# RWKV time mixing on one core: a drain with two pairs of denominator banks and a log that runs one tile ahead, replaced by a drain with one pair of banks and the log and exponential of a tile in direct succession

## The chip, the cores and the metric

The kernel runs on one core of a Trainium2 chip. The metric is the device time of one execution in microseconds (us). Five engines work beside each other, each in its own program order: TensorE (PE, matmul, with its weight loads shown as PEld), VectorE (DVE), ScalarE (ACT), GpSimd (POOL) and SyncE (SP). SP, ACT and POOL also issue transfers between the on-chip memory (SBUF) and the main memory; the queues of those issues are shown as SPq, ACTq and POOLq. Matmul results lie in PSUM, eight banks of 128 x 512 float32.

## The reference

The inputs are `k` and `v` of shape (16, 2048, 256) and the vectors `w` (decay) and `u` (bonus) of length 256. For each of the 16 sequences and each of the 256 channels a recurrence runs over 2048 steps, and all of it is in float32:

```python
for t in range(seq_len):
    ww = u + kk; qq = max(pp, ww)
    e1, e2 = exp(pp - qq), exp(ww - qq)
    output[b, t] = (e1 * aa + e2 * vv) / (e1 * bb + e2 + 1e-08)
    ww = pp - w + kk; qq = max(ww, kk)
    e1, e2 = exp(ww - qq), exp(kk - qq)
    aa, bb, pp = e1 * aa + e2 * vv, e1 * bb + e2, qq
```

So each output is a ratio of a weighted sum of `v` (the numerator) to the sum of the weights (the denominator), and the state `aa, bb, pp` is carried from step to step.

## The kernel before

**Tiles.** The 2048 steps are cut into 16 chunks of 128 steps (`NST = 16`), and the 16 sequences into four groups of four. A tile `n` is one group in one chunk, so there are `NP = 64` tiles, numbered chunk by chunk: tile `n` belongs to chunk `n // 4`. A tile holds 128 steps (the partitions) by 1024 numbers (4 sequences x 256 channels), computed in two halves `i = 0, 1` of 512 columns.

**One tile's work.** `logs(n)` (PE) builds exponents from `k` in PSUM; `exps(n)` (ACT, L204) turns them into weights and writes them to a ring in SBUF, `EZR`, that has room for 12 tiles; `times_v(n)` (DVE, L214) multiplies them by `v`. `sums(n)` (PE, L238) adds up what the chunk contributes to the state. Ten turns later (`LAG = 10`) the output side of the same tile runs:

- `den(n)` (PE, L341): four matmuls of 512 columns, which leave the denominators of both halves in a pair of PSUM banks, `DENB` (banks 4 and 5).
- the reciprocal (ACT): the natural log of the pair into an SBUF tile `rd` (`den_log`, L346, 128 x 1024), and the exponential of the negated log, in place (`den_exp`, L349, 128 x 1024).
- `num(n, bank, i)` (PE, L358): two matmuls of 512 columns for each half, which leave the numerator in one bank.
- `mult(n, bank, i)` (DVE, L362): numerator times reciprocal, into `rd`.
- `store(n)` (SP, L365): `rd` (512 KB) to the output in main memory. There are eight `rd` tiles, so the log of tile `n` needs the store of tile `n - 8` to have landed.

**The state.** After the last tile of a chunk the state goes through a chain of small steps: `copy_sums` (out of PSUM), `turn` (PE, L255, a transposition by matmul), `state_logs` (ACT, L260), `state_frames`, `state_scan` and `state_offsets` (on DVE in the last chunk, L269 to L286), `state_weights` (ACT, L290), `state_chain` (DVE, L299 to L304), `turn_back` (PE, L320), and `inject` (DVE copy L326, then four transfers of 8 KB, L331), which writes the incoming state into rows of `EZR`. The output side of the next four tiles reads these rows: `den` needs the first two of the four transfers, `num` the other two. For the last chunk (`c = 15`) these are the tiles 60 to 63.

**Order.** All instructions are kept in the order of the program (`K(...)`), so each engine's queue is written out by hand. In the steady loop (`for n in range(LAG, NP)`) the small steps are slotted in by a table, `later`, of (turn, place, step), called by `small_work`. In the last turn of that loop `n = 63`, and the output side has come to tile `q = 53`.

**The drain.** What follows the loop handles the outputs of the tiles 53 to 63 and the state chain of chunk 15, with no loads and no weights left to compute. In the kernel before it is written out line by line:

- Denominators alternate between two pairs of banks (`dbank`: banks 2 and 3, or `DENB`), so that `den(n + 1)` is computed while the log of tile `n` still reads the other pair. Numerators go round three single banks (`nbank`: 0, 1 and 6).
- On ACT the log runs one tile ahead: log(n + 1), then exp(n), then log(n + 2), and so on. No two neighbours depend on each other.
- The steps of the state chain stand between the first few tiles at places of their own; `inject(c, SP)` issues its four transfers on SP's queue.
- The products and the store of a tile come as soon as its reciprocal is there (`outputs`): two products of 512 columns, then the store.
- Of tile 63 the log is taken whole; then, for each half, exponential, product, and two transfers of 128 KB, one on SP's queue and one on ACT's (L533). ACT issues its transfer of the first half ahead of the exponential of the second.

Of the kernel before, what the change touches and what calls it, by code (L numbers as in the profile page):

```python
# [7 lines left out]
F32 = mybir.dt.float32  # L8
# [3 lines left out]
ACT = mybir.ActivationFunctionType  # L12
# [3 lines left out]
def kernel(  # L16
# [14 lines left out]
    TC = 2 * HS  # L31
# [22 lines left out]
    def rows_of(x, n):  # L54
        c, p = divmod(n, 4)
        return x[4 * p:4 * p + 4, c * TC:(c + 1) * TC, :].rearrange("n t d -> t n d")
# [114 lines left out]
    def ez(n):  # L171
        return EZR[:, :, n % RING]
# [6 lines left out]
    def logs(n):  # L179
        km = KM[n].rearrange("p (i n) d -> p i (n d)", i=2)  # L180

        def rows(q):
            for i in range(2):
                g = 32 * (2 * q + i)
                K(PE.matmul(half(n, q)[:, i, :], CO[g:g + 32, :],  # L185
                            WU[g:g + 32, :].unsqueeze(1).broadcast_to([32, 2, Dm]), start=True, stop=False,
                            tile_position=(g, 0), skip_group_check=True))

        def steps(q):
            for i in range(2):  # L190
                K(PE.matmul(half(n, q)[:, i, :], (NLE, NLZ)[q], km[:, i, :], start=False, stop=True,  # L191
                            skip_group_check=True))

        rows(0)
        rows(1)
        steps(0)
        steps(1)
# [33 lines left out]
    def sums(n):  # L231
        c, p = divmod(n, 4)
        t = MISC[:, 0:Dm]
        for o in range(2):
            x = 24 - 16 * o - 2 * p
            for j in range(4):
                q, i = divmod(j, 2)
                K(PE.matmul(t[32 * j:32 * j + 32, :], mats["OH"][:, x:x + 32],  # L238
                            ez(n)[:, 2 * q, i, Dm * o:Dm * o + Dm],
                            start=p == 0 and o == 0, stop=p == 3 and o == 1,  # L240
                            tile_position=(0, 32 * j), skip_group_check=True))
# [79 lines left out]
                        skip_group_check=True))  # L321
        st[c, "CT"] = t

    def inject(c, queue=POOL):
        cb = small.tile([128, 128], BF16, tag="cb", name="cb")
        K(DVE.tensor_copy(cb, st.pop((c, "CT"))))  # L326
        r0 = 4 * c % RING
        for q in range(2):
            for h in range(2):
                r, x = HS * h + HS - 1, 32 * (2 * q + h)  # L330
                K(queue.dma_start(  # L331
                    out=EZR[r:r + 1, 2 * q, r0:r0 + 4, :, :].rearrange("o p i (b x) -> o (p i b) x", b=4),
                    in_=cb[x:x + 32, :]))


    RD = {}

    def den(n, bank=DENB):
        for m, q in (("L", 0), ("Id", 1)):
            for i in range(2):  # L340
                K(PE.matmul(bank[:, i, :], mats[m], ez(n)[:, q, i, :], start=q == 0, stop=q == 1,  # L341
                            skip_group_check=True))

    def den_log(n, bank=DENB):
        RD[n] = rpool.tile([128, 2, D], F32, tag="rd", name="rd")
        K(SC.activation(RD[n], bank, ACT.Ln, scale=RS))  # L346

    def den_exp(n, i=slice(0, 2)):
        K(SC.activation(RD[n][:, i, :], RD[n][:, i, :], ACT.Exp, scale=-1.0))  # L349

    def recip(n, between):
        den_log(n)
        between()
        den_exp(n)

    def num(n, bank, i):
        for m, q in (("LN", 2), ("IdN", 3)):
            K(PE.matmul(bank, mats[m], ez(n)[:, q, i, :], start=q == 2, stop=q == 3, skip_group_check=True))  # L358

    def mult(n, bank, i):  # L360
        rd = RD[n]
        K(DVE.tensor_mul(rd[:, i, :], bank, rd[:, i, :]))  # L362

    def store(n):
        K(SP.dma_start(out=rows_of(out, n), in_=RD.pop(n).rearrange("p i (n d) -> p (i n) d", n=2)))  # L365

    later = {}
    for c in range(NST):
        s = 4 * c + 3
        plan = [(s + 1, "act" if s + 1 < LAG else "recip", copy_sums), (s + 1, "pe", turn),  # L370
                (s + 2, "act", state_logs), (s + 2, "mid", state_frames), (s + 2, "scan", state_scan), (s + 2, "scan", state_offsets),
                (s + 3, "recip", state_weights), (s + 3, "chain", state_chain),
                (s + 4, "nums", turn_back), (s + 4, "mid", inject), (s + 4, "mid", state_next)]
        if c == 0:
            plan = [(s + 1, "act", copy_sums), (s + 1, "pe", turn), (s + 1, "pe", state_logs),
                    (s + 1, "round", state_frames), (s + 1, "round", state_scan), (s + 1, "round", state_offsets),
                    (s + 2, "act", state_weights), (s + 2, "round", state_chain),
                    (s + 3, "pe", turn_back), (s + 3, "round", inject), (s + 3, "round", state_next)]
        if c == 1:
            plan = [(s + 1, "act", copy_sums), (s + 1, "pe", turn), (s + 2, "act", state_logs),  # L380
                    (s + 2, "round", state_frames), (s + 2, "round", state_scan), (s + 2, "round", state_offsets),
                    (s + 3, "recip", state_weights), (s + 3, "early", state_chain)] + plan[8:]
        if c == NST - 1:
            plan = []
        for slot, where, f in plan:
            later.setdefault((slot, where), []).append((f, c))

    def small_work(n, where):
        for f, c in later.pop((n, where), []):
            f(c)  # L390
# [35 lines left out]
    def inverses(n):  # L426
        q, qp = n - LAG, n - LAG - 1
        if qp >= 0:
            num(qp, NUMB, 1)

        sums(n - 1)
        if n + 1 < NP:
            recip(q, lambda: small_work(n, "recip"))

    for n in range(LAG, NP):

        q, qp = n - LAG, n - LAG - 1
        load(n + AHEAD)

        if qp >= 2:  # L440
            store(qp - 2)
        if qp >= 0:
            num(qp, NUMB, 0)
        den(q)
        small_work(n, "nums")
        exps(n)
        small_work(n, "act")
        if qp >= 0:
            mult(qp, NUMB, 0)
        small_work(n, "mid")  # L450
        if n == LAG:

            inverses(n)
            small_work(n, "early")
        if n + 2 < NP:
            round_k(n + 2)

        if n % 4 in (3, 0):
            cast_v(n)
        if n + 1 == NP:  # L460
            times_v(n)
        elif n % 4 < 2:
            cast_v(n + 1)
        if n > LAG:
            inverses(n)
        if qp >= 0:
            mult(qp, NUMB, 1)
        small_work(n, "scan")
        if n + 1 < NP:
            times_v(n)  # L470
            small_work(n, "chain")
            logs(n + 1)
        small_work(n, "pe")

    q, c = NP - LAG - 1, NST - 1
    dbank = lambda n: PS[:, 2:4, :] if (n - q) % 2 else DENB
    nbank = lambda n, i: PS[:, (0, 1, 6)[(2 * (n - q) + i) % 3], :]  # L480
    tile_num = lambda n, i: num(n, nbank(n, i), i)

    def outputs(n):
        for i in range(2):
            mult(n, nbank(n, i), i)
        store(n)

    den_log(q)
    den(q + 1, dbank(q + 1))
    sums(NP - 1)  # L490
    copy_sums(c)
    store(q - 2)
    store(q - 1)
    den_exp(q)
    den_log(q + 1, dbank(q + 1))
    tile_num(q, 0)
    turn(c)
    state_logs(c)
    den_exp(q + 1)
    den(q + 2, dbank(q + 2))  # L500
    den_log(q + 2, dbank(q + 2))
    tile_num(q, 1)
    mult(q, nbank(q, 0), 0)
    state_frames(c)
    state_scan(c)
    state_offsets(c)
    state_weights(c)
    mult(q, nbank(q, 1), 1)
    store(q)
    state_chain(c)  # L510
    den(q + 3, dbank(q + 3))
    for i in range(2):
        tile_num(q + 1, i)
    turn_back(c)
    inject(c, SP)
    outputs(q + 1)
    for n in range(q + 2, NP):
        if n + 1 < NP:
            den_log(n + 1, dbank(n + 1))
        if n + 2 < NP:  # L520
            den(n + 2, dbank(n + 2))
        for i in range(2):
            tile_num(n, i)
        if n + 1 < NP:
            den_exp(n)
            outputs(n)
    n, p = NP - 1, (NP - 1) % 4
    for i in range(2):
        den_exp(n, slice(i, i + 1))
        mult(n, nbank(n, i), i)  # L530
        for j, eng in ((0, SP), (1, SC)):
            b = 4 * p + 2 * i + j
            K(eng.dma_start(out=out[b, c * TC:(c + 1) * TC, :], in_=RD[n][:, i, Dm * j:Dm * j + Dm]))  # L533
    assert not later


# [28 lines left out]
```

## Time and profile before

| | us |
|---|---|
| median of 3 runs (lowest, highest) | 290.13 (289.65, 290.43) |
| the profiled execution, its own time | 289.65 |
| its span, first to last instruction | 288.0 |
| mean granted TensorE clock | 0.988 |
| busy: PE, DVE, ACT, POOL | 261.4, 262.3, 254.7, 105.2 |
| start of the log (L346) of tile 53, of tile 54 | 258.54, 260.56 |
| end of the last product (L362) | 284.15 |

The profile is one execution, read by a hardware profiler. A row of the timeline gives start and length in us, the engine, the line of the kernel, what is written from what, and in square brackets how long the engine had been idle and who released it. The rows of "windows" give a stretch, its length, each engine's busy time (with its number of instructions), the granted TensorE clock as a share of full speed, the busy share of the 16 DMA engines and the rate in GB/s. The page's second part cuts the span into 40 slices of 7.2 us and gives tenths of busy time for each. The profiled execution's time is 1.65 us more than its span.

### The profile page before, as it was taken

To read this page: it belongs to the slowest core of one execution; us is meant where nothing else is said; L and a number is where in the kernel's file an instruction comes from. 1 tells how busy PE (TensorE), PEld (TensorE's weight loads), DVE (VectorE), ACT (ScalarE), POOL (GpSimd) and SP (SyncE) were. 2 spreads that over 40 slices of the span, in tenths; PEclk is the share of its full clock that TensorE was granted. 3 is DMA by queue.
4 is the path that set the end of the run, shared out by engine and by line. 5 is a ranking of instruction groups with operands and counts; after the bars stand their busy time and mean duration, and the time that the engine had idled before them with its cause. 6 is when DMAs were issued, how large, how long until landed. Compare 5 with 4: busy or idle time off the path is not lost. (4 is left out here: it accounts for less than half of the span.)

```text
span 288.0 us, 5023 instructions
## 1 busy us (share of the span) xinstructions
PE 261.4 (91%) x1694; PEld 119.4 (41%) x1694; DVE 262.3 (91%) x463; ACT 254.7 (88%) x252; POOL 105.2 (37%) x208
## 2 busy tenths in 40 slices
PE   5997897999999999999999999899998989998990
PEld 1443443544444544435444444344344444433430
DVE  4698999999999999999999999998999999988863
ACT  2675678999999999999999989999998999998891
POOL 7000523352534454543525364460434435233000
PEclk9799999999999999999999999999999999999997
DMA  6999999999999999999999999999999999994697
GB/s 214 353 348 350 349 331 349 331 361 375 381 369 381 372 379 378 381 379 381 378 376 381 369 381 375 377 376 371 373 374 380 374 377 380 373 383 160 201 339 245
DMA packets 103587, 101.54 MB, mean 353 GB/s; under 512 B 4285, under 2 KB 103561, under 8 KB 103561
## 3 DMA queue, kind: packets, MB, share of 16 engines
q1 hardware_dynamic: 101336, 100.45, 102.6%
q0 software_dynamic: 1920, 0.50, 0.8%
q8 instruction: 13, 0.21, 0.3%
q10 hardware_dynamic: 304, 0.27, 0.3%
q14 instruction: 14, 0.11, 0.1%
HBM read 67.12 MB, written 33.55 MB: 350 GB/s over the span
## 5 line engine op out<-in xcount | busy, mean ns | idle before, releaser
L204 ACT ACTIVATE EZR<-PS 128x2048 bf16<-128x2048 f32 x54 | 101.2, 1875 | 7.5 <-PE PS L191 6.5
L362 DVE TENSOR_TENSOR rd<-PS,rd 128x512 f32<-128x512 f32 x128 | 87.0, 687 | 6.1 <-ACT rd L349 4.7
L214 DVE TENSOR_TENSOR EZR<-EZR,vb 128x2048 bf16<-128x2048 bf16 x64 | 78.1, 1220 | 2.2 <-ACT EZR L202 1.5
L349 ACT ACTIVATE rd<-rd 128x1024 f32<-128x1024 f32 (+1 forms) x65 | 67.9, 1047 | 2.7 <-DVE rd L362 1.8
L346 ACT ACTIVATE rd<-PS 128x1024 f32<-128x1024 f32 x64 | 65.7, 1026 | 0.8 <-PE PS L341 0.8
L358 PE MATMUL PS<-EZR,LN 128*128 128x512 bf16 x128 | 48.7, 381 | 12.2 <-DVE rd L362 8.4
L331 POOL DMA_DIRECT2D EZR<-cb x60 | 36.5, 614 | 52.1 <-DVE cb L326 45.4
L176 DVE CAST km<-kr 128x1024 fp32r<-128x1024 f32 x64 | 44.7, 699 | 6.9 <-DMA kr<-in_k_dram 6.4
L191 PE MATMUL PS<-km,NLE 128*128 128x512 f32 x128 | 47.5, 453 | 2.3 <-DVE km L176 2.2
L358 PE MATMUL PS<-EZR,IdN 128*128 128x512 bf16 x128 | 48.4, 378 | 0.0
L209 DVE CAST vb<-vr 128x1024 bf16<-128x1024 f32 x64 | 43.4, 694 | 0.7 <-DMA vr<-in_v_dram 0.7
L191 PE MATMUL PS<-km,NLZ 128*128 128x512 f32 x128 | 40.6, 398 | 0.0
L341 PE MATMUL PS<-EZR,Id 128*128 128x512 bf16 x128 | 38.1, 379 | 0.0
L341 PE MATMUL PS<-EZR,L 128*128 128x512 bf16 x128 | 38.1, 379 | 0.0
L185 PE MATMUL PS<-WU,CO 32*128 32x512 bf16 x256 | 27.2, 388 | 3.4 <-DVE WU L400 2.2
L269 POOL TENSOR_TENSOR F<-LL,LL 128x32 f32<-128x32 f32 x13 | 6.7, 515 | 61.9 <-ACT LL L260 61.9
L191 PEld LDWEIGHTS PS<-km,NLZ 128*128 128x128 f32 x128 | 24.4, 191 | 5.8
L191 PEld LDWEIGHTS PS<-km,NLE 128*128 128x128 f32 x128 | 19.3, 190 | 17.3 <-issue 12.9
L238 PE MATMUL PS<-EZR,OH 128*32 128x256 bf16 x512 | 26.1, 278 | 0.1
L202 ACT ACTIVATE EZR<-PS 128x1024 bf16<-128x1024 f32 x20 | 19.4, 1019 | 7.6 <-PE PS L191 7.6
L358 PEld LDWEIGHTS <-IdN 128*128 128x128 bf16 x128 | 12.5, 97 | 28.7 <-issue 26.3
L282 POOL TENSOR_TENSOR Q<-P,F 128x64 f32<-128x64 f32 x13 | 15.7, 1205 | 15.0 <-DVE P L273 15.0
(71 smaller groups left out, 200.0 us busy)
## 6 DMA issues: line engine op xcount, KB each, us to landing
kr<-in_k_dram SPq DMA_DIRECT2D x64, 512.0 KB, 8.3
vr<-in_v_dram SPq DMA_DIRECT2D x64, 512.0 KB, 8.3
out_dram<-rd SPq DMA_DIRECT2D x63, 512.0 KB, 8.1
EZR<-cb POOLq DMA_DIRECT2D x60, 8.0 KB, 5.3
out_dram<-rd SPq DMA_DIRECT2D x2, 128.0 KB, 2.7
out_dram<-rd ACTq DMA_DIRECT2D x2, 128.0 KB, 2.2
EZR<-cb SPq DMA_DIRECT2D x4, 8.0 KB, 1.9
wuf<-in_w_dram ACTq DMA_DIRECT2D x1, 8.0 KB
```

The costliest lines, as they stand in the source:

```text
L176: K(DVE.tensor_copy(km, kr_of.pop(n)))
L185: K(PE.matmul(half(n, q)[:, i, :], CO[g:g + 32, :], WU[g:g + 32, :].unsqueeze(1).broadcast_to([32, 2, Dm]), start=True, stop=False, tile_p ...
L191: K(PE.matmul(half(n, q)[:, i, :], (NLE, NLZ)[q], km[:, i, :], start=False, stop=True, skip_group_check=True))
L204: K(SC.activation(ez(n)[:, 0:2], PS[:, 0:4, :].rearrange("p (q i) x -> p q i x", q=2), ACT.Exp))
L209: K(DVE.tensor_copy(vb, vr))
L214: K(DVE.tensor_mul(ez(n)[:, 2:4], ez(n)[:, 0:2], vb.unsqueeze(1).broadcast_to([128, 2, 2, D])))
L331: K(queue.dma_start(out=EZR[r:r + 1, 2 * q, r0:r0 + 4, :, :].rearrange("o p i (b x) -> o (p i b) x", b=4), in_=cb[x:x + 32, :]))
L341: K(PE.matmul(bank[:, i, :], mats[m], ez(n)[:, q, i, :], start=q == 0, stop=q == 1, skip_group_check=True))
L346: K(SC.activation(RD[n], bank, ACT.Ln, scale=RS))
L349: K(SC.activation(RD[n][:, i, :], RD[n][:, i, :], ACT.Exp, scale=-1.0))
L358: K(PE.matmul(bank, mats[m], ez(n)[:, q, i, :], start=q == 2, stop=q == 3, skip_group_check=True))
L362: K(DVE.tensor_mul(rd[:, i, :], bank, rd[:, i, :]))
```

## The change

Up to the end of the steady loop the kernel stays as it is, apart from the output side of its last turn, which now calls the whole reciprocal of tile 53 there and issues `den(54)` at its end. The written-out drain goes, and a loop over `n = 64 ... 74` takes its place, with `q = n - 10` the tile whose reciprocal is taken and `qp = n - 11` the tile whose numerator is computed:

- one pair of denominator banks, `DENB`, for all tiles: `den(q + 1)` stands behind `num(qp)` and writes the pair that the log of tile `q` reads;
- `recip(q)`: log and exponential of one tile follow each other on ACT; for tile 63 they go half by half (log, exp, log, exp);
- numerators alternate between two pairs of banks, 0 and 1, or 2 and 3 (`H`), with one product of 1024 columns for both halves (tile 63: two of 512);
- the state chain of chunk 15 is slotted in by the table: `state_logs` behind the exponential of tile 54, `state_weights` behind that of tile 55, `state_chain` after it, `turn_back` behind `num(55)`, `inject` on POOL's queue, and the products of the tiles 54 and 55 behind the copy of `inject`;
- the transfers of the last tile are issued behind both of its exponentials.

There are 10 products fewer (two of 512 columns become one of 1024 for each of the tiles 53 to 62) and one log more (tile 63).

```diff
-    def inject(c, queue=POOL):
+    def inject(c):
...
-    def den(n, bank=DENB):
+    def den(n):
...
-    def den_log(n, bank=DENB):
-        RD[n] = rpool.tile([128, 2, D], F32, tag="rd", name="rd")
-        K(SC.activation(RD[n], bank, ACT.Ln, scale=RS))
-    def den_exp(n, i=slice(0, 2)):
-        K(SC.activation(RD[n][:, i, :], RD[n][:, i, :], ACT.Exp, scale=-1.0))
+    def recip(n, between=lambda: None):
+        rd = rpool.tile([128, 2, D], F32, tag="rd", name="rd")
+        for i in (slice(0, 1), slice(1, 2)) if n == NP - 1 else (slice(0, 2),):
+            K(SC.activation(rd[:, i, :], DENB[:, i, :], ACT.Ln, scale=RS))
+            between()
+            K(SC.activation(rd[:, i, :], rd[:, i, :], ACT.Exp, scale=-1.0))
+        RD[n] = rd
...
+    def last_outputs(n, H):
+        c, p = divmod(n, 4)
+        for i in range(2):
+            mult(n, H[:, i, :], i)
+            for j, eng in ((0, SP), (1, SC)):
+                b = 4 * p + 2 * i + j
+                K(eng.dma_start(out=out[b, c * TC:(c + 1) * TC, :], in_=RD[n][:, i, Dm * j:Dm * j + Dm]))
...
         if c == NST - 1:
-            plan = []
+            plan = [(s + 1, "copy", copy_sums), (s + 1, "turn", turn),
+                    (s + 1, "post", state_logs), (s + 1, "mid", state_frames), (s + 1, "mid", state_scan), (s + 1, "mid", state_offsets),
+                    (s + 2, "post", state_weights), (s + 2, "first", state_chain),
+                    (s + 3, "turn", turn_back), (s + 3, "first", inject)]
...
+        else:
+            den(q + 1)
         small_work(n, "pe")
-    q, c = NP - LAG - 1, NST - 1
-    dbank = lambda n: PS[:, 2:4, :] if (n - q) % 2 else DENB
-    nbank = lambda n, i: PS[:, (0, 1, 6)[(2 * (n - q) + i) % 3], :]
-    tile_num = lambda n, i: num(n, nbank(n, i), i)
-    def outputs(n):
-        for i in range(2):
-            mult(n, nbank(n, i), i)
-        store(n)
-    den_log(q)
-    den(q + 1, dbank(q + 1))
-    sums(NP - 1)
-    copy_sums(c)
-    store(q - 2)
-    store(q - 1)
-    den_exp(q)
-    den_log(q + 1, dbank(q + 1))
-    tile_num(q, 0)
-    turn(c)
-    state_logs(c)
-    den_exp(q + 1)
-    den(q + 2, dbank(q + 2))
-    den_log(q + 2, dbank(q + 2))
-    tile_num(q, 1)
-    mult(q, nbank(q, 0), 0)
-    state_frames(c)
-    state_scan(c)
-    state_offsets(c)
-    state_weights(c)
-    mult(q, nbank(q, 1), 1)
-    store(q)
-    state_chain(c)
-    den(q + 3, dbank(q + 3))
-    for i in range(2):
-        tile_num(q + 1, i)
-    turn_back(c)
-    inject(c, SP)
-    outputs(q + 1)
-    for n in range(q + 2, NP):
-        if n + 1 < NP:
-            den_log(n + 1, dbank(n + 1))
-        if n + 2 < NP:
-            den(n + 2, dbank(n + 2))
-        for i in range(2):
-            tile_num(n, i)
-        if n + 1 < NP:
-            den_exp(n)
-            outputs(n)
-    n, p = NP - 1, (NP - 1) % 4
-    for i in range(2):
-        den_exp(n, slice(i, i + 1))
-        mult(n, nbank(n, i), i)
-        for j, eng in ((0, SP), (1, SC)):
-            b = 4 * p + 2 * i + j
-            K(eng.dma_start(out=out[b, c * TC:(c + 1) * TC, :], in_=RD[n][:, i, Dm * j:Dm * j + Dm]))
+    sums(NP - 1)
+    small_work(NP, "copy")
+    late = []
+    store(NP - LAG - 3)
+    store(NP - LAG - 2)
+    for n in range(NP, NP + LAG + 1):
+        q, qp = n - LAG, n - LAG - 1
+        H = PS[:, 2 * (n % 2):2 * (n % 2) + 2, :]
+        for i in range(2):
+            num(qp, H[:, i, :], i)
+        small_work(n, "turn")
+        if q < NP:
+            recip(q, lambda: small_work(n, "recip"))
+        small_work(n, "post")
+        if q + 1 < NP:
+            den(q + 1)
+        small_work(n, "first")
+        if qp == NP - 1:
+            last_outputs(qp, H)
+            break
+        late.append((qp, H))
+        if n != NP + 1:
+            for x, bank in late:
+                mult(x, bank, slice(0, 2))
+                store(x)
+            late = []
+        small_work(n, "mid")
```

More of the change, by code (lines that the diff above doesn't have):

```diff
@@ L330, in inject @@
                 r, x = HS * h + HS - 1, 32 * (2 * q + h)
-                K(queue.dma_start(
+                K(POOL.dma_start(
                     out=EZR[r:r + 1, 2 * q, r0:r0 + 4, :, :].rearrange("o p i (b x) -> o (p i b) x", b=4),
@@ L336 @@
     RD = {}
-    def den(n, bank=DENB):
+    def den(n):
         for m, q in (("L", 0), ("Id", 1)):
             for i in range(2):
-                K(PE.matmul(bank[:, i, :], mats[m], ez(n)[:, q, i, :], start=q == 0, stop=q == 1,
+                K(PE.matmul(DENB[:, i, :], mats[m], ez(n)[:, q, i, :], start=q == 0, stop=q == 1,
                             skip_group_check=True))
-    def den_log(n, bank=DENB):
-        RD[n] = rpool.tile([128, 2, D], F32, tag="rd", name="rd")
-        K(SC.activation(RD[n], bank, ACT.Ln, scale=RS))
-    def den_exp(n, i=slice(0, 2)):
[L349 to L353, printed above, removed]
-        den_exp(n)
+    def recip(n, between=lambda: None):
[5 more added lines that the diff above has]
+        RD[n] = rd
     def num(n, bank, i):
@@ L431, in inverses @@
         sums(n - 1)
-        if n + 1 < NP:
-            recip(q, lambda: small_work(n, "recip"))
+        recip(q, lambda: small_work(n, "recip"))
     for n in range(LAG, NP):
@@ L515 @@
-    inject(c, SP)
-    outputs(q + 1)
-    for n in range(q + 2, NP):
-        if n + 1 < NP:
-            den_log(n + 1, dbank(n + 1))
-        if n + 2 < NP:
-            den(n + 2, dbank(n + 2))
-        for i in range(2):
-            tile_num(n, i)
-        if n + 1 < NP:
-            den_exp(n)
-            outputs(n)
-    n, p = NP - 1, (NP - 1) % 4
-    for i in range(2):
-        den_exp(n, slice(i, i + 1))
-        mult(n, nbank(n, i), i)
-        for j, eng in ((0, SP), (1, SC)):
-            b = 4 * p + 2 * i + j
-            K(eng.dma_start(out=out[b, c * TC:(c + 1) * TC, :], in_=RD[n][:, i, Dm * j:Dm * j + Dm]))
+    sums(NP - 1)
@@ new lines @@
+    small_work(NP, "copy")
[5 more added lines that the diff above has]
+        H = PS[:, 2 * (n % 2):2 * (n % 2) + 2, :]
+        for i in range(2):
+            num(qp, H[:, i, :], i)
+        small_work(n, "turn")
+        if q < NP:
+            recip(q, lambda: small_work(n, "recip"))
+        small_work(n, "post")
[12 more added lines that the diff above has]
+        small_work(n, "mid")
```

## The prediction

> **What bounds the kernel now.** The change leaves everything up to the last turn of the steady loop as it is, so I read only the last 30 us: first the page's slices, then the windows of the drain, then its timeline, then its last five rows.
>
> The page's slices, in tenths of busy time:
>
> ```profile
> ACT  2675678999999999999999989999998999998891
> DMA  6999999999999999999999999999999999994697
> GB/s 214 353 348 350 349 331 349 331 361 375 381 369 381 372 379 378 381 379 381 378 376 381 369 381 375 377 376 371 373 374 380 374 377 380 373 383 160 201 339 245
> ```
>
> In the last four slices (259 us on) ACT stays busy, while the DMA engines first fall to 160 GB/s and then come back to 339. The windows show why:
>
> ```profile
> 266.00:270.40 4.40, 4.39 (x24) 2.15 (x25) 3.56 (x7) 3.64 (x5) 0.00 (x0) 1.00 0.37 118
> 270.40:285.90 15.50, 10.30 (x46) 4.25 (x44) 9.43 (x15) 11.18 (x13) 0.00 (x0) 0.95 1.02 338
> 285.90:288.00 2.10, 0.00 (x0) 0.00 (x0) 0.00 (x0) 0.00 (x0) 0.00 (x0) 0.50 0.03 8
> ```
>
> From 270.4 to 285.9 the DMA engines are full (share 1.02) at 338 GB/s: 15.5 us x 338 = 5.24 MB, the ten stores of tiles 54 to 63. Nothing but the end of the program follows, 2.1 us. The set of the pace is in the timeline (rows of PE, ACT and the SP queue):
>
> ```profile
> 258.54 1.02 ACT L346 ACTIVATE rd<-PS 128x1024 f32<-128x1024 f32 x1
> 259.59 1.06 ACT L349 ACTIVATE rd<-rd 128x1024 f32<-128x1024 f32 x1
> ...
> 266.01 0.40 PE L320 MATMUL PS<-Id,CB 128*128 128x128 bf16 x4 [0.72 <-DVE CB L304]
> 266.25 0.59 PE L341 MATMUL PS<-EZR,L 128*128 128x512 bf16 x2
> 266.68 0.59 PE L341 MATMUL PS<-EZR,Id 128*128 128x512 bf16 x2
> 266.77 2.52 SPq L331 DMA_DIRECT2D EZR<-cb  x4
> 267.31 1.02 ACT L346 ACTIVATE rd<-PS 128x1024 f32<-128x1024 f32 x1 [0.76 <-PE PS L341]
> 268.23 1.05 ACT L349 ACTIVATE rd<-rd 128x1024 f32<-128x1024 f32 x1
> 269.18 1.01 ACT L346 ACTIVATE rd<-PS 128x1024 f32<-128x1024 f32 x1
> 269.39 12.80 SPq L365 DMA_DIRECT2D out_dram<-rd  x9
> 270.08 1.06 ACT L349 ACTIVATE rd<-rd 128x1024 f32<-128x1024 f32 x1
> 271.03 1.02 ACT L346 ACTIVATE rd<-PS 128x1024 f32<-128x1024 f32 x1
> ```
>
> Four prices come from here. Independent neighbours on ACT overlap: log to exp 0.90 (269.18 to 270.08), exp to log 0.95, so a tile takes 1.85. An exp that needs the log just before it starts 1.05 after it (258.54 to 259.59). A `den` takes 266.68 + 0.59 - 266.25 = 1.02 from first start to last end, and frees PE after 0.86. A hand-over takes 0.04 (267.27 to 267.31). The L346 rows from 267.31 on are the logs of tiles 57, 58, ... 63 (278.43). The end:
>
> ```profile
> 280.46 1.89 DVE L362 TENSOR_TENSOR rd<-PS,rd 128x512 f32<-128x512 f32 x3 [0.57 <-ACT rd L349]
> 281.82 0.37 SPq L365 DMA_DIRECT2D out_dram<-rd  x1
> 282.38 0.36 ACTq L533 DMA_DIRECT2D out_dram<-rd  x1
> 282.80 0.63 ACT L349 ACTIVATE rd<-rd 128x512 f32<-128x512 f32 x1 [1.84 <-DVE rd L362]
> 283.46 0.69 DVE L362 TENSOR_TENSOR rd<-PS,rd 128x512 f32<-128x512 f32 x1 [1.11 <-ACT rd L349]
> ```
>
> Store 62 is issued at 281.82; data end at 285.95 (the finer windows), 4.13 later: 1.04 from issue to data, and 3.09 for 1.05 MB (tiles 62 and 63) at 339 GB/s. The last product, 284.15, is not late: its pieces find the queue full. So **end of span = issue of store 62 + 4.13 + 2.05**, which gives 288.0, as long as the queue behind store 62 does not run dry. What the change does to that one instruction is what I work out.
>
> **The change, step by step.**
>
> *Start, tiles 53 to 57.* `den(54)` now waits for log(53), which ends at 259.56; with 0.04, 1.02 and 0.04 its own log starts at 260.67 instead of 260.56. The state chain moves more. `state_logs` stands behind exp(54) instead of ahead of it: 261.72 + 0.95, and `turn` too is later since both halves of `num(53)` (0.43 more) precede it; about 262.7 instead of 262.31. On DVE the whole product of tile 53 stands ahead of `state_frames`: it starts at 262.2 and occupies 1.14 (two halves took 0.61 each, a doubled column count adds 512 / 0.96 GHz, an estimate from L214's 1.22 for its 2048 columns of two to a cycle), so the frames start at 263.3 instead of 262.69. They are ready by 264.9, but `state_weights` (264.33 before) stands behind exp(55), which starts at 264.67: 265.6. That is 1.3 late, and the chain behind it keeps its 1.6 on DVE, so `turn_back` goes from 266.01 to 267.2. `den(57)` is queued behind it on PE as `den(56)` is in the row above, so log(57) starts at 268.5 instead of 267.31: **1.2 late**, ACT idle 0.6.
>
> *Two products held back.* The products of 54 and 55 stand behind the copy of `inject`, which ends at 267.9; that of 54 ends at 269.2. `num(56)` writes the same banks, so it waits until 269.2 and holds PE to 270.1; `den(58)` is queued behind it, though log(57) was done at 269.5. Log(58) starts at 270.07 + 1.03 + 0.04 = 271.14 instead of 269.18: **1.96 late**.
>
> *Pace.* From here a `den` needs the log before it to end (one bank pair), and that log's successor needs the `den`: 1.02 + 0.04 + 1.03 + 0.04 = 2.13 a tile instead of 1.85; ACT alone would need 1.05 + 0.95 = 2.00, so PE's turn is what sets it. Log(62) is four tiles on: 271.14 + 8.52 = 279.66 instead of 276.58, **3.08 late**.
>
> *Back at the end.* Before, exp(62) stands behind log(63); now it comes straight after its own log, so the product waits for `num(62)` instead. That is queued behind `den(63)`, which waits for log(62): 279.66 + 1.02 + 0.04 = 280.72, PE free at 281.58, `num(62)` done at 282.61, product 282.65 to 283.87 (before 281.75). So store 62 is issued 283.94 instead of 281.82: **2.12 late**.
>
> *Tile 63.* Log(63) starts at 281.8, its four half passes end at 284.3, the last product at 285.1 (the 1.84 us that ACT waited with its transfer ahead of the exponential are gone). The last 256 KB could be out by 285.1 + 1.1 + 0.77 = 287.0; the queue behind store 62 runs until 283.94 + 4.13 = 288.07, which is later. So tile 63's gain is worth nothing here.
>
> *Queue of the injection.* On SP the four issues took 2.52 and landed 1.9 after issue; SP's store of tile 54 stood behind them (269.39, though its product ended at 267.9). On POOL four took 2.06 in the main part and landed 3.5 after issue in the last stretch (5.3 in the page's median). Issued from about 268.2, the two that `den(60)` needs land at 272.3 by the one figure, 274.1 by the other; `den(60)` is due at 274.3 (log(59) ends). Cost 0, with 0 to 0.2 of room by the worse figure. Cover that goes would cost 1 us for each us.
>
> *Sum.* Data end 288.07, span 290.1: **+2.1**. The profiled execution would be 289.65 + 2.1 = 291.75; the runs' median is 0.48 above it, so 290.13 + 2.1 = **292.2**.
>
> A rule that would make it less: the Trainium skill, "DMA: Bandwidth & Descriptors", section "Anatomy of one DMA", gives 2.0 us plus bytes / 436 GB/s for one transfer. By it the 1.05 MB behind store 62 would take 2.4 us, not 3.09, and the difference between the kernels would be about 1.5 us. The windows' 338 GB/s over 15.5 us is the measurement, and I stay with it. The section "Issuing engine by pattern" says that transfers issued by SP or ACT are generally faster than by GpSimd; the rows agree (1.9 against 3.5), and I let it cost nothing only because of the room above.
>
> Bounds: a hand-over of 0.02 or 0.10 instead of 0.04 moves the sum to 1.9 or 2.5 (two a tile); the wide product, not in the trace, at 1.05 (one pass, no fixed part) or 1.3 (no saving at all) moves it to 1.9 or 2.4.
>
> **The rivals.**
>
> *Write-out sets the end anyway (same).* The ten stores need 15.5 us from the first on. If the tiles come no slower than that, the end hangs on store 54 alone, issued at 269.2 in place of 269.39: span 287.9, 290.0 in all. It needs a pace near 1.55 to 1.85. For: DMA is full now. Against: 2.13 a tile leaves the queue dry between stores (1.55 each).
>
> *SP freed and exp(62) early (faster).* If the chain is not late and `den` is hidden, store 54 leaves at 267.95 instead of 269.39, and the ten stores end 1.4 sooner: 288.7. It decides if the logs keep 1.85 from log(57) on; exp(62) comes before log(63), so products are ready 0.9 sooner, which the queue could use. Against: one bank pair, and a `den` of 1.02 can't lie beside the log that reads it.
>
> *Injection late (slower still).* If the landing from POOL is the page's 5.3 and issues are as late as their worst, `den(60)` waits and everything behind it; 1 us late gives 293.2.
>
> **How the numbers follow.** My forecast 0.76, injection late 0.09, same 0.09, faster 0.06. The forecast's own range is 291.5 to 292.9 (bounds above with 0.3 of spread in the runs). 8 in 10 need a little of each side: 290.9 to 293.2. About 0.3%, 0.87 us, is what can be told from no change: faster than 289.26, slower than 291.00. Slower: 0.76 + 0.09, faster 0.06, same 0.09.
>
> **What would show it.** In the changed profile: log to log 2.1 from tile 58 on, each with PE's `den` as releaser; log(58) near 271.1; gaps in DMA between 275 and 284, then full for the last 3 us; store 62 near 283.9; last product near 285.1. Wrong if the logs step by 2.0 or less, if `turn_back` is no later than 266.5, or if the DMA engines are full throughout.

## The result, and the profile after

The changed kernel takes 291.13 us (median of 4 runs, 290.98 to 291.18) against 289.89 us for the kernel before in the same comparison: ratio 1.0041, 95% interval 1.0022 to 1.0061, so 0.2% to 0.6% slower. The forecast was 292.2, +2.1 us; the runs show +1.24. The profiled execution took 290.98 us, with a span of 289.3 us (before: 288.0).

Where the time went is read from the last 31 us. The windows of the drain, kernel after (columns as before; the last three are the granted TensorE clock, the DMA share and GB/s):

```profile
266.00:270.40 4.40, 3.02 (x17) 1.38 (x17) 3.80 (x7) 3.63 (x4) 2.01 (x4) 1.00 0.19 62
270.40:276.00 5.60, 4.94 (x22) 1.97 (x21) 3.28 (x4) 5.15 (x5) 0.00 (x0) 1.00 1.01 328
276.00:284.00 8.00, 6.52 (x28) 2.62 (x27) 5.27 (x5) 7.48 (x10) 0.00 (x0) 1.00 0.79 269
284.50:287.50 3.00, 0.00 (x0) 0.00 (x0) 0.26 (x1) 0.00 (x0) 0.00 (x0) 1.00 1.02 341
287.50:289.30 1.80, 0.00 (x0) 0.00 (x0) 0.00 (x0) 0.00 (x0) 0.00 (x0) 0.77 0.04 14
```

The DMA engines are full only until 276, run at 0.79 while the tiles come too slowly to feed them, and are full again for the last 3 us, when the stores of tiles 62 and 63 meet. The timeline of the kernel after shows what feeds them (rows of PE and ACT; the first is log(53)):

```profile
258.44 1.02 ACT L347 ACTIVATE rd<-PS 128x1024 f32<-128x1024 f32 x1
...
266.91 0.40 PE L320 MATMUL PS<-Id,CB 128*128 128x128 bf16 x4 [0.73 <-DVE CB L304]
267.14 0.59 PE L341 MATMUL PS<-EZR,L 128*128 128x512 bf16 x2
...
268.20 1.02 ACT L347 ACTIVATE rd<-PS 128x1024 f32<-128x1024 f32 x1 [0.62 <-PE PS L341]
268.82 0.38 PE L354 MATMUL PS<-EZR,LN 128*128 128x512 bf16 x1 [0.65 <-DVE rd L358]
...
270.74 1.02 ACT L347 ACTIVATE rd<-PS 128x1024 f32<-128x1024 f32 x1 [0.42 <-PE PS L341]
...
271.81 0.59 PE L341 MATMUL PS<-EZR,L 128*128 128x512 bf16 x2 [0.25 <-ACT rd L347]
...
272.88 1.02 ACT L347 ACTIVATE rd<-PS 128x1024 f32<-128x1024 f32 x1
```

`turn_back` waits for the state chain and `den(57)` stands behind it, so ACT is idle for 0.62 before log(57); `num(56)` waits 0.65 for a product that is held back, and before log(58) ACT is idle again, for 0.42. Then each `den` waits for the log before it (0.25 at 271.81), and the logs stand 2.14 apart. The end of the kernel after (rows of DVE and the issuing queues):

```profile
282.33 2.42 DVE L358 TENSOR_TENSOR rd<-PS,rd 128x1024 f32<-128x1024 f32 x3 [0.91 <-PE PS L354]
283.59 0.37 SPq L361 DMA_DIRECT2D out_dram<-rd  x1
284.19 1.32 SPq L369 DMA_DIRECT2D out_dram<-rd  x2
284.19 1.36 ACTq L369 DMA_DIRECT2D out_dram<-rd  x2
```

The product of tile 62 had waited 0.91 for its numerator. Store 62 is issued at 283.59, and 5.69 us later the span ends.

All profiles below are compared on one scale. Nothing ahead of log(53) differs between the kernels, but log(53) itself starts anywhere from 257.66 to 260.23 in the 14 profiles; so each time is counted from the start of log(53) in its own timeline (258.54 before, 258.44 after). "turn_back" is the start of the last of its four matmuls, "tail" the time from the issue of store 62 to the end of the span. The places are those of one profiled execution each; the ratio is that of the timed runs, each against runs of the kernel before in its own comparison.

| kernel | turn_back | log(58) | log(62) | store 62 | last product ends | tail | span ends | ratio to before (95%) |
|---|---|---|---|---|---|---|---|---|
| before | 7.65 | 10.63 | 18.04 | 23.27 | 25.61 | 6.14 | 29.41 | 1 |
| after | 8.65 | 12.30 | 20.84 | 25.15 | 26.32 | 5.69 | 30.84 | 1.0041 (1.0022 to 1.0061) |
| before, one bank pair | 7.84 | 11.28 | 19.83 | 25.31 | 27.64 | 5.99 | 31.30 | 1.0072 (1.0054 to 1.0089) |
| after, two pairs | 9.58 | 14.12 | 22.13 | 25.61 | 27.24 | 5.67 | 31.28 | 1.0040 (1.0021 to 1.0059) |
| after, two pairs, denominators first | 8.66 | 11.06 | 19.07 | 22.54 | 24.17 | 5.88 | 28.42 | 0.9960 (0.9946 to 0.9975) |
| after, products not held | 8.65 | 11.91 | 20.45 | 24.76 | 25.93 | 5.69 | 30.45 | 1.0040 (1.0026 to 1.0055) |
| after, chain early | 8.20 | 11.86 | 20.40 | 24.71 | 25.88 | 5.67 | 30.38 | 1.0031 (1.0019 to 1.0043) |
| after, both of these | 8.19 | 11.79 | 20.33 | 24.64 | 25.81 | 5.68 | 30.31 | 1.0040 (1.0022 to 1.0057) |
| after, injection on SP | 8.65 | 12.30 | 20.85 | 25.15 | 26.32 | 5.95 | 31.11 | 1.0052 (1.0038 to 1.0066) |
| before, no store 58 | 7.64 | 10.63 | 18.03 | 23.27 | 25.61 | 5.95 | 29.22 | 1.0006 (0.9995 to 1.0016) |
| before, new end | 7.66 | 10.64 | 18.04 | 22.62 | 24.00 | 7.00 | 29.61 | 1.0006 (0.9989 to 1.0023) |
| before, injection on POOL | 7.66 | 10.64 | 18.04 | 23.28 | 25.62 | 5.62 | 28.90 | 0.9996 (0.9978 to 1.0014) |
| before, both of these | 7.65 | 10.63 | 18.04 | 22.61 | 23.99 | 5.89 | 28.50 | 0.9970 (0.9957 to 0.9983) |
| the last, and den(57) first | 7.64 | 10.33 | 17.75 | 22.32 | 23.70 | 5.94 | 28.26 | 0.9956 (0.9940 to 0.9971) |

By this scale the change costs 30.84 - 29.41 = 1.43 us: store 62 is 1.88 us later and the tail is 0.45 shorter. The 1.88 is 1.67 at log(58), 1.13 more by log(62) (four steps of 2.135 instead of 1.853), less 0.92 behind it.

### The profile page after: what moved, and what is told of

It reads as the page before. It is cut to its first block, busy times and chain, and to the rows that moved or that the text cites. A ratio compares the mean times of both kernels' runs of the same rounds, so it can differ in the third digit from the quotient of the medians.

```text
span 289.3 us, 5011 instructions
## 1 busy us (share of the span) xinstructions
PE 263.1 (91%) x1694; PEld 119.7 (41%) x1694; DVE 261.8 (90%) x453; ACT 256.2 (89%) x253; POOL 109.9 (38%) x212
## 5 line engine op out<-in xcount | busy, mean ns | idle before, releaser
L358 DVE TENSOR_TENSOR rd<-PS,rd 128x512 f32<-128x512 f32 (+1 forms) x118 | 86.2, 733 | 6.8 <-PE PS L354 5.7
L347 ACT ACTIVATE rd<-PS 128x1024 f32<-128x1024 f32 (+1 forms) x65 | 65.8, 1012 | 1.5 <-PE PS L341 1.3
L331 POOL DMA_DIRECT2D EZR<-cb x64 | 38.8, 612 | 56.3 <-DVE cb L326 43.2
L191 PE MATMUL PS<-km,NLZ 128*128 128x512 f32 x128 | 41.2, 404 | 0.0
```

The source lines that it names most:

```text
L331: K(POOL.dma_start(out=EZR[r:r + 1, 2 * q, r0:r0 + 4, :, :].rearrange("o p i (b x) -> o (p i b) x", b=4), in_=cb[x:x + 32, :]))
L347: K(SC.activation(rd[:, i, :], DENB[:, i, :], ACT.Ln, scale=RS))
```

## The experiments

**One pair of denominator banks, alone, in the kernel before.**

```diff
-    dbank = lambda n: PS[:, 2:4, :] if (n - q) % 2 else DENB
+    dbank = lambda n: DENB
```

> The kernel before with one edit: all denominators in one pair of banks (the log still runs one tile ahead). Theory of the forecast (the pace sets the store of tile 62, and the end follows 4.0 after it): from tile 56 on the logs step by 2.13 instead of 1.85, log(63) is about 2.0 us late, store 62 about 2.0 us late, the time about +2.0 us. Rival, the write-out of ten stores sets the end (15.5 us from store 54 on): at most +0.3 us. Rival, the late state chain is what costs: 0, since the chain stays where it is.

Store 62 came 2.04 us later and the span's end 1.89 us; the logs step by 2.14. The timeline of this kernel has the wait itself:

```profile
277.77 0.59 PE L341 MATMUL PS<-EZR,L 128*128 128x512 bf16 x2 [0.25 <-ACT rd L346]
...
279.90 0.59 PE L341 MATMUL PS<-EZR,L 128*128 128x512 bf16 x2 [0.25 <-ACT rd L346]
```

The bank pair alone, with the log still a tile ahead and the chain where it was (`turn_back` 0.19 later), sets a step of 2.14: the order of log and exponential isn't what makes it. Both rivals (at most 0.3, and 0) fall; the timed runs are 0.7% slower.

**Two pairs of banks, in the kernel after.** The denominators alternate as before; with banks 2 and 3 taken, the numerators go round the three single banks again.

```diff
-            num(qp, H[:, i, :], i)
+            num(qp, nbank(qp, i), i)
...
-            recip(q, lambda: small_work(n, "recip"))
+            recip(q, lambda: small_work(n, "recip"), dbank(q))
...
-            den(q + 1)
+            den(q + 1, dbank(q + 1))
...
-        if n != NP + 1:
+        if True:
-                mult(x, bank, slice(0, 2))
+                for i in range(2):
+                    mult(x, nbank(x, i), i)
```

> The kernel after with two pairs of denominator banks and three single numerator banks, as before, and, since these need it, products in halves and the products of tile 54 not held back. Log and exponential still follow each other. Theory of the forecast: logs step by 2.00 (1.05 + 0.95) instead of 2.13, and the numerator of tile 62 no longer stands behind a waiting den(63): product 62 and store 62 about 1.9 us earlier than in the kernel after, the time about -1.7 us against after, so +-0.4 of the kernel before. Rival, the chain and the held products cost it all: -0.5 us against after at most.

The step fell to 2.00 and from log(62) to store 62 it took 3.48 instead of 4.31, both as the theory has it, and yet the end came 0.44 us later than in the kernel after, and the timed runs show no gain at all (1.0040 against 1.0041). The rest was lost at the start, and the timeline names a new wait:

```profile
265.87 1.31 DVE L360 TENSOR_TENSOR rd<-PS,rd 128x512 f32<-128x512 f32 x2
266.64 0.38 PE L356 MATMUL PS<-EZR,LN 128*128 128x512 bf16 x1 [2.08 <-DVE rd L360]
266.86 0.38 PE L356 MATMUL PS<-EZR,IdN 128*128 128x512 bf16 x1
267.07 0.39 PE L320 MATMUL PS<-Id,CB 128*128 128x128 bf16 x4
```

The second half of `num(55)` falls into the bank of the first half of `num(54)`, whose product stands behind the state chain on DVE (265.87). PE stood still for 2.08 us, with `turn_back` and `den(57)` queued behind: `turn_back` 0.93 later, log(58) 1.82 later than in the kernel after. Part of the 1.82 is a lower TensorE clock behind the wait, shown in the last section. My expectation left out this wait on the numerators' bank.

**The same, denominators and `turn_back` ahead of the numerators.** From turn 65 on `den(q + 1)` and `turn_back` are issued before `num(qp)`.

```diff
+        if n > NP:
+            if q + 1 < NP:
+                den(q + 1, dbank(q + 1))
+            small_work(n, "turn")
         for i in range(2):
             num(qp, nbank(qp, i), i)
...
-        if q + 1 < NP:
+        if n == NP:
             den(q + 1, dbank(q + 1))
```

> As a_two_pairs, but from turn 65 on the denominators of the next tile and turn_back stand ahead of the numerators on PE. If a_two_pairs lost its gain because num(55) waited for the product of tile 54 with turn_back and den(57) queued behind it: turn_back back to 8.65 us after log(53) or earlier (9.58 in a_two_pairs), log(58) near 11.1 (14.12), logs 2.00 apart, store 62 near 22.6 (25.61), drain near 28.3 us (31.28), time about -1 us against before. Rival, two pairs leave too few numerator banks whatever the order: log(58) stays above 13.

`turn_back` 8.66, log(58) 11.06, steps of 2.00, store 62 at 22.54, end 28.42: each within 0.12 us of what was expected. So the lost gain was that one wait and what was queued behind it, not the number of banks. This kernel is faster than the one before, though log and exponential follow each other and its state chain is a microsecond later: it is still 1.03 us behind at log(62), and makes that good in the 3.47 us from there to store 62, which take 5.23 before.

**The held-back products, and the late chain, each alone and together, in the kernel after.**

```diff
-        if n != NP + 1:
+        if True:
```

> The kernel after with one edit: the product of tile 54 comes in its own turn, behind the state chain, not behind the copy of the injection. Theory of the forecast (it priced the held products at 0.75 us: log(58) 1.96 late against 1.2 for log(57)): num(56) starts about 268.1 instead of 268.82, log(58) about 270.3 instead of 270.74, -0.4 us at the end; the injection is issued about 0.7 us later and still lands ahead of den(60). Rival, nothing hangs on it since the write-out sets the end: 0.

```diff
-                    (s + 1, "post", state_logs), ...
-                    (s + 2, "post", state_weights), ...
+                    (s + 1, "recip", state_logs), ...
+                    (s + 2, "recip", state_weights), ...
```

> The kernel after with one edit: the two ACT steps of the state chain stand between log and exponential of tiles 54 and 55, not behind the exponential. Theory of the forecast: turn_back 0.5 us earlier (266.4 instead of 266.91), the held products and log(58) with it, -0.5 us at the end. Rival, the chain lies beside other work: 0; or the exponentials pushed back by 0.3 us each cost as much as the chain gains: 0 to +0.3.

Log(58) came 0.39 and 0.44 us earlier, the end 0.39 and 0.46. Both of them together:

> The kernel after with the edits of a_no_hold and a_chain_early together. Each alone gave 0.39 and 0.46 us. If both only remove waits in front of den(58), which after that hangs on log(57) (2.14 behind it): log(58) at 11.8 us after log(53), 0.5 us gained in all. Rival, the two costs add: log(58) at 11.45, 0.85 us gained.

Log(58) at 11.79, the end 0.53 us earlier. The two costs do not add: they are two waits in front of one `den(58)`, and once either is gone it waits for log(57), which is then 2.14 to 2.19 ahead. Log(57) itself comes only 0.10 to 0.12 earlier with the early chain, for the steps of the chain between log and exponential put log(56) 0.50 later. With both waits gone log(58) is still 1.16 later than in the kernel before. The steps are small against the spread of the timed runs (the ratios of these three and of the kernel after lie within each other's intervals); the reading rests on the profiles, one of each, where the places lie within 0.25 us of the expected ones.

**The queue of the injection, in the kernel after.** The four transfers go back to SP's queue.

> The kernel after with one edit: the four transfers of the last injection on SP's queue, as before. Theory of the forecast (POOL costs nothing, the end hangs on store 62): store 54 is issued at about 270.2 instead of 268.79, the queue catches up by tile 58, end 0 (within 0.2 us). Rival, the injection from POOL lands late and holds den(60): -0.3 us or more. Rival, the write-out sets the end: +1.4 us.

All places up to the last product are the same to 0.01, so the injection from POOL holds nothing. (In the kernel after, the two transfers that `den(60)` needs had landed at 271.78, and `den(60)` started at 273.95.) The span ends 0.27 later with SP, all of it in the tail. From the landing of the last transfer to the end of the span it is 1.50 us in this kernel and 1.55 before, but 1.21 after: with the injection on SP the closing work behind the last landing is longer, which I had not expected. All 14 profiles divide this way: 1.48 to 1.73 us in the five kernels with the last injection on SP, 1.08 to 1.21 in the nine with it on POOL. Why it is so was not settled.

**No store of tile 58, in the kernel before** (these rows of the output stay unwritten).

> The kernel before without the store of tile 58 (its rows of the output are not written). Theory of the forecast (end = issue of store 62 + 4.1 + 2.05, the queue has no backlog when store 62 comes): 0, at most -0.2 us, with a gap of about 1.5 us in the DMA windows around 277. Rival, the write-out of ten stores sets the end: -1.5 us.

The end came 0.19 us earlier, not 1.5. The windows of this kernel show the gap where the store was:

```profile
270.10:276.50 6.40, 6.40 (x32) 2.87 (x30) 4.33 (x8) 6.40 (x8) 0.00 (x0) 1.00 0.99 328
276.50:277.50 1.00, 1.00 (x6) 0.49 (x5) 1.00 (x2) 1.00 (x2) 0.00 (x0) 1.00 0.66 227
277.50:285.50 8.00, 2.83 (x11) 0.87 (x9) 4.09 (x7) 3.76 (x5) 0.00 (x0) 0.95 0.88 298
```

The timed runs show no difference (1.0006). Full DMA engines over 15.5 us look like the only bound, but 512 KB fewer moved the end by 0.19 only: from the issue of store 62 to the last landing it takes 4.58 us before and 4.47 here, so the backlog that store 62 found in the queue was 0.11 us, and the rest is shorter closing work. In the kernel before two limits stand side by side: the full queue, and right behind it the issue of store 62.

**The end and the queue, in the kernel before.** Three kernels: the end as in the kernel after; the injection on POOL; both.

```diff
-        if n + 1 < NP:
+        if n + 1 < NP - 1:
             den_log(n + 1, dbank(n + 1))
...
+    RD[n] = rpool.tile([128, 2, D], F32, tag="rd", name="rd")
     for i in range(2):
+        K(SC.activation(RD[n][:, i, :], dbank(n)[:, i, :], ACT.Ln, scale=RS))
         den_exp(n, slice(i, i + 1))
+    for i in range(2):
         mult(n, nbank(n, i), i)
```

> The kernel before with the end of the kernel after: exp(62) ahead of the log of tile 63, log and exponential of tile 63 by halves, the last transfers behind both exponentials. Last product about 1.6 us earlier (282.4 instead of 284.15), store 62 about 0.65 earlier. Theory that the queue behind the stores sets the end: ten stores from 270.45 on still need 15.4 us, so the data end 0 to 0.2 us earlier, time 0 to -0.2. Rival, the engines set the end: -1.2 to -1.6 us.

```diff
-    inject(c, SP)
+    inject(c)
```

> The kernel before with one edit: the four transfers of the last injection on POOL's queue. Store 54 leaves at about 9.45 us after log(53) instead of 10.84. If store 62 decides: store 62 stays at 23.27, and only the small backlog that store 62 found in the queue goes (0.19 by the run without store 58) and the later end of SP's closing list (0.27 by a_inj_sp): drain 28.9 to 29.2 instead of 29.41, and most of b_tail_inj's gain needs both edits. Rival, the whole gain of b_tail_inj (0.9) is the injection's: 28.5.

> As b_tail, and the four transfers of the last injection on POOL's queue, so that store 54 leaves when its product is done (about 268.0 instead of 269.39). Theory that the queue sets the end: now store 62 (0.65 earlier) decides, -0.4 to -0.65 us against before. Rival, the engines set the end: as b_tail, no difference between the two. Rival, POOL lands too late: slower than b_tail.

With the new end alone the last product ends 1.6 us earlier and store 62 is issued 0.65 earlier, but the span's end is 0.20 later. Its windows:

```profile
270.40:273.00 2.60, 2.60 (x13) 1.18 (x12) 1.77 (x3) 2.60 (x4) 0.00 (x0) 1.00 0.96 318
273.00:278.00 5.00, 5.00 (x25) 2.28 (x24) 3.76 (x6) 5.00 (x7) 0.00 (x0) 1.00 1.03 340
278.00:283.00 5.00, 2.72 (x10) 0.84 (x9) 3.88 (x7) 3.82 (x6) 0.00 (x0) 1.00 1.03 339
```

Here the queue binds: full from the first store to the last, and the earlier product only waits in it (tail 7.00). The last transfer lands 27.88 us after log(53), as in the kernel before (27.86); the 0.20 is closing work. With the injection on POOL alone, store 54 leaves 1.38 us earlier (9.46 against 10.84) and the end comes 0.51 earlier. With both it is 0.91, where the two alone give -0.20 and +0.51 (in the timed runs 0.9970 against 1.0006 and 0.9996). Part of that is the closing work, 1.14 and 1.08 with the injection on POOL against 1.55 before. Counted to the landing of the last transfer the new end alone gives -0.02, the injection on POOL alone 0.09 (about the backlog), both 0.44: an earlier end of the engines' work pays only after the queue has been started earlier.

**A version that beats both.** As the last, and `den(57)` issued ahead of `turn_back`.

```diff
+    den(q + 4, dbank(q + 4))
     turn_back(c)
...
-        if n + 2 < NP:
+        if q + 2 < n < NP - 2:
             den(n + 2, dbank(n + 2))
```

> As b_tail_inj, and den(57) is issued ahead of turn_back instead of behind it, so that PE does it while it waits for the state chain. If the end hangs on store 62 and on the queue behind store 54 together: log(57) 0.87 us earlier (7.9 us after log(53) instead of 8.77), store 62 at about 21.75 after log(53) instead of 22.61, drain (log(53) to the end of the span) about 27.7 us instead of 28.50 for b_tail_inj and 29.41 before, time -1.7 us against before. Rival, the queue alone binds (store 54 leaves as in b_tail_inj): 28.3 to 28.5, no gain on b_tail_inj.

288.59 us against 290.06 in its comparison, ratio 0.9956 (0.9940 to 0.9971): faster than the kernel before and than the kernel after, though not told apart by the runs from the kernel that it builds on (0.9970, 0.9957 to 0.9983). Log(57) came at 7.88, as expected, but log(58) at 10.33, where steps of 1.85 would put it at 9.73; of the 0.8 us expected over the previous kernel 0.24 came. The timeline has the wait that took the place of the one removed:

```profile
267.69 0.38 PE L358 MATMUL PS<-EZR,LN 128*128 128x512 bf16 x1 [0.55 <-DVE rd L362]
...
269.18 1.02 ACT L346 ACTIVATE rd<-PS 128x1024 f32<-128x1024 f32 x1 [0.48 <-PE PS L341]
```

The second half of `num(55)` waits for the product of tile 54, which stands behind the copy of the injection on DVE, and `den(58)` is queued behind it: the held product again.

## Why the prediction was right, and where it was off

The direction, the range (290.9 to 293.2) and most of the mechanism held; the size was too large, +2.1 against 1.24 in the medians and 1.43 between the profiles. Of what is missing between +2.12 and 1.43, 0.24 is store 62 (1.88 late, not 2.12), the rest the tail behind it.

- **Pace: right.** 2.13 was forecast, 2.14 measured; one bank pair alone gives the same step and two pairs 2.00.
- **Back at the end: right.** 0.96 to be gained between log(62) and store 62 (3.08 late against 2.12), 0.92 measured; the product of tile 62 waits for its numerator behind `den(63)`, as the 0.91 in its row shows.
- **Start: over-sized, 1.96 against 1.67.** The term for the chain put `turn_back` 1.2 late; it was 1.00. Exp(55), and with it `state_weights`, was put at 264.67, 6.13 after log(53); it started 5.84 after it (264.28), since PE was through with `turn` sooner and with `den(55)` behind it: `turn` started 0.26 later than before, not 0.43, and its row is 0.58 long after, against 0.69 before. Log(57) was 1.00 late, not 1.2. The held products were put at 0.76 on top of that, and 0.67 was measured (1.67 - 1.00); but only 0.39 of it is the hold, the rest is one step more at the pace of the single bank pair. The forecast gave the whole start to the chain and the hold. The runs show the bank pair close behind them: alone it puts log(58) 0.65 late, and with the hold gone and the chain early 1.16 of the 1.67 remain.
- **Tail: taken as constant, 4.13 + 2.05 = 6.18; it is 6.14 before and 5.69 after.** This is the step that failed. Up to the last landing the 4.58 before were 4.47 after: 0.11 was backlog in the queue, though the forecast assumed that store 62 found none. Behind the last landing it took 1.55 before and 1.21 after: with the injection on SP the closing work is longer (by 0.27 in the kernel after with that one edit), and I had priced the queue of the injection at 0. The change takes both away. 1.88 - 0.45 = 1.43 closes the sum.
- **Wide product:** my 1.14 to the next start leant on a clock figure that no row here shows; the rows have it right all the same: 1.23 long, with the next start 1.14 later (262.00 to 263.14).
- **Tile 63's gain worth nothing: right, for the reason given.** In the kernel after the DMA engines are full from 284.5 to 287.5, and the last product ends at 284.76, as this stretch begins. In the new end alone, where the queue is full throughout, the last product came 1.6 earlier and the span ended no sooner.
- **The rule set against the sum** (the Trainium skill, "DMA: Bandwidth & Descriptors", "Anatomy of one DMA": 2.0 us plus bytes / 436 GB/s, a fit for transfers issued from GpSimd) was put at +1.5, nearer to the result than +2.1, but not for its reason: the last full windows after run at 341 GB/s, before at 338. Nor does +1.5 follow from it, since a shorter time for the same last 1.05 MB would shorten both kernels alike.
- **A slip in reading:** the `den` at 266.25 in the rows shown of before is `den(57)`, not `den(56)`; it stands behind `turn_back` in both kernels, so the difference that I formed is the right one.

## What to carry to other kernels

Find the one instruction behind which only a fixed amount of work is left (here the issue of the last large store), and follow each edit to that instruction; then ask what the edit does to the amount itself, which went from 6.14 to 5.69 us here. Gains on the far side of that instruction, such as a last tile finished earlier, are worth nothing while the queue is full. A DMA queue that is full to the end need not be the only bound: leave one transfer out and see how far the end moves before the next limit holds it. And when a buffer is split or shared anew, ask what each in-order engine has queued behind the instruction that now waits: the same two bank pairs (with products in halves, not held back) brought nothing in the timed runs in one order of PE's instructions, and 2.42 us of the drain in another.

## What the runs showed of the hardware

In the kernel with two pairs PE stood still for 2.08 us, and a little over a microsecond after it had started again the granted clock fell, to 0.55 in the mean of the next 3.8 us (windows of that kernel, clock in the third column from the right):

```profile
266.60:267.70 1.10, 1.06 (x8) 0.61 (x8) 0.79 (x2) 0.21 (x1) 0.00 (x0) 1.00 0.00 0
267.70:271.50 3.80, 3.80 (x11) 1.40 (x10) 2.67 (x5) 2.08 (x2) 2.00 (x4) 0.55 0.81 266
271.50:273.00 1.50, 1.50 (x9) 0.69 (x7) 0.74 (x2) 1.20 (x2) 0.00 (x0) 1.00 0.72 237
```

In that stretch PE was busy all the time, and its matmuls of 512 columns took 0.63 us instead of 0.38; the wait cost more than its own length, for log(57) to log(58) took 2.98 us there and 2.00 in the kernel with the denominators first. Waits of 0.73 us in the kernel after (266.91) and of 0.98 us in the kernel with the denominators first left the clock at 1.00.

Whether a pause is followed by a fall differs from one execution to the next. At about 46 us, in a part that all kernels share, PE waits in every one of the 14 profiles, for 1.52 to 1.85 us. In four of them (in the table "after, chain early", "after, both of these", "after, injection on SP" and "before, new end") the clock fell to half around the end of that pause, for 3.4 to 6.8 us; in the other ten it did not, though the pause was as long in two of them. Two of the fourteen, each with the row that ends the pause and the window behind it, first "after, chain early", then "after, two pairs, denominators first":

```profile
45.98 0.38 PE L354 MATMUL PS<-EZR,LN 128*128 128x512 bf16 x1 [1.85 <-DVE rd L358]
46.50:50.00 3.50, 3.50 (x19) 1.66 (x19) 2.56 (x4) 0.98 (x2) 2.86 (x6) 0.51 1.09 347
...
45.47 0.38 PE L356 MATMUL PS<-EZR,LN 128*128 128x512 bf16 x1 [1.85 <-DVE rd L360]
45.50:49.00 3.50, 3.50 (x24) 1.57 (x24) 3.50 (x6) 2.26 (x3) 2.72 (x6) 1.00 1.09 349
```

So the 0.44 us by which the kernel with two pairs ends later than the kernel after is that of an execution with the fall. Its twelve timed runs suggest that not every one has it, though a mean clock does not say where a fall lay: five lie from 289.96 to 290.12 us, at mean clocks of 0.984 to 0.997, six from 291.37 to 292.33, at 0.969 to 0.980, and the profiled one at 290.67 and 0.975. The Trainium skill, "TensorE: Matmul & The Clock Gate", Part 1, has the clock set by how busy PE was in a free-running window of about 3.4 us, which fits a fall that comes with some delay and after one pause of 1.85 us but not after another; its section "HAM oscillation" names idle gaps of more than that length as what to avoid, and here 2.08 us, and in four profiles 1.84 or 1.85, was enough.

The drain itself repeats closely: log(58) and log(62) agree to 0.01 us in the five kernels that leave them untouched (10.63 or 10.64, 18.03 or 18.04). So the spread of the timed runs must lie mostly ahead of it, where log(53) started anywhere from 257.66 to 260.23 us; what makes that spread was not looked into.
